# Weight sums of the retention's value and gate projections: by accumulating loads in place of vector additions, with the seven products reordered

## The chip, the cores and the metric

The kernel runs on one core of a Trainium2 chip. Its metric is the device time of one execution in microseconds. The engines named below are PE (the matrix engine), DVE (vector), ACT (activations), POOL and SP; SP issues the loads and stores of the kernel before.

## The reference

Two layers over 1024 tokens of width 1024, in float32. The first is a retention with four heads, each with 256 query and key columns and 512 value and gate columns; the second is a stick-breaking attention with eight heads. Cut to what the change touches, the first layer is:

```python
u = rms_norm(h, ret_norm_pre[i])
proj = u @ ret_w_in[i]
q, k, v, g = jnp.split(proj, [...], axis=-1)
q = rope(split_heads(q)); k = rope(split_heads(k)) * (RET_QK_DIM ** -0.5)
o = retention_chunkwise(q, k, v)
o = (o - mu) * lax.rsqrt(var + EPS)
o = merge_heads(o) * jax.nn.silu(g)
y = o @ ret_w_out[i]
h = h + rms_norm(y, ret_norm_post[i])
```

The change is in how `v` and `g` are computed from `u` and their weights.

## The kernel before, in words

The tokens are taken in two halves of 512. The retention is done for each half in turn (phases A, t = 0 and 1), then the attention for each half (phases C). Every float32 operand of a matmul is kept as two tiles of reduced precision, a high and a low part; `split` (L574) makes them with one ACT copy (L577) and one DVE subtraction (L578), and `mm3` (L412) issues three matmuls (L415, L416, L417) for a product. A load of weights brings 128 partitions of 512 floats, 256 KB, into a raw tile (`raw_w`, L342, a ring of six `wraw` buffers in phases A); two such raw tiles are split into one block of weights in a `whl` tile, of which there are three.

In a phase A each head u runs three main pieces of work: `qk`, the projection to queries and keys; the output projection of the head before (`outproj`); and `vg` (L770), the projection to values and gates. `vg` runs for seven of the eight heads (the first head of the first half uses plain projections). `vg` splits the tokens of the half (256 and 256), the 1024 input columns (512 and 512) and the output columns (values and gates) each in two, and computes the 2 by 2 block product with seven block products instead of eight. The products are numbered 1 to 7. Each has two weight blocks, i = 0 and 1, and each block serves two K tiles of 128 and two token blocks: 12 matmuls a block, 24 a product. Some products take a loaded block of weights as it is (1, 2, 4), others sums of blocks, made by DVE before the split: for product 5 the sum of two gate blocks (L797), for 6 that sum less a value block (L800), for 3 a value block less the last sum (L803), for 7 a gate block less that sum (L806). The running sum lies in the two `S` tiles (L781). The tokens' sums are made once per half by `sums` (L630).

The products share PSUM banks. Products 1, 6 and 7 accumulate in one pair of banks, 5 and 3 in a second pair, 2 in a third and 4 in a fourth; after a product whose bank goes on accumulating, ACT copies the bank out (`copy`, L821), and `plus` (L825) adds such a copy to another bank's content, which gives the values (`vput`) and gates (`gput`). The order of the products is written out at L828 as 1, 2, 5, 6, 3, 7, 4.

Beside a main piece run side pieces: `scores` (query times key, masked by POOL at L892), `mix` (scores times values, with a normalisation whose small steps run on POOL at L938, L939 and L940) and `gate` (product with the gates, transposed by PE at L983). The order of every engine's queue is not the program's: `arrange` (L101) simulates all engines with a cost per instruction (`_time`, L68), tries five rounds of priorities (`latest`, `justify`, `place`), and fixes the best order found on all five queues. Each queue then runs in order, each instruction waiting for what it needs.

Of the kernel before, what the change touches and what calls it, by code (L numbers as in the profile page):

```python
# [37 lines left out]
BACKLOG = 3000.0  # L38
HAND = {"PE": 100.0, "DVE": 60.0, "Activation": 60.0, "Pool": 100.0, "SP": 50.0}
# [28 lines left out]
def _time(s, chip):  # L68

    n = _size(s.outs[0])  # L70
    if s.eng == "PE":
        full = str(s.ins[0].dtype) == "dt.float32" and not s.turns
        t = max(216.0, n * 5 / 3 + 26.0) if full else max(110.0, n / 2.4 + 13.5)
        return t, t + 165.0
    bank = any(b.tensor.name in chip.banks for b in s.ins)
    if s.eng == "DVE":
        two = sum(_size(b) == n for b in s.ins) > 1
        if s.op == "InstTensorTensor":
            t = (n + 143) / 0.96
# [18 lines left out]
    return n * 512 / 330.0, 4000.0  # L98


def arrange(nc, tc, tag_of, bufs, banks, turns):  # L101
# [4 lines left out]
    for ins in nc.cur_bb.bb.instructions:  # L106
# [8 lines left out]
        s.turns = bool(getattr(ins, "is_transpose", False))  # L115
        s.before, s.after, s.behind, s.next = set(), set(), set(), set()
# [21 lines left out]
        s.shares = s.eng == "Pool" or s.eng == "DVE" and sum(b.tensor.name not in banks for b in s.ins) > 1  # L138
# [45 lines left out]
def justify(steps, order, follow):  # L184
# [8 lines left out]
    for s in sorted(steps, key=lambda s: (-s.end, -s.k)):  # L193
# [9 lines left out]
        busy = max(s.busy, 400.0) if s.eng == "SP" else s.busy  # L203
# [11 lines left out]
def place(steps, users, tags, tag_of, bufs, rank):  # L215
# [41 lines left out]
    for _ in range(n):  # L257
# [51 lines left out]
def trunk(ctx, tc, xT, wts, gains, trig, ident_in, cols, out):  # L309
# [52 lines left out]
    keep = tc.keep_in_program_order  # L362
# [121 lines left out]
    def outproj(base, oT, y_d, first, acc=None, tags=None):  # L484
# [11 lines left out]
        def chunk(j):  # L496
# [110 lines left out]
    def a_prep(t):  # L607
# [22 lines left out]
        def sums(i):  # L630
# [95 lines left out]
    class AHead:  # L726
# [19 lines left out]
        def gput(self, tb, src):  # L746
            g = self.sg[tb] = S("sg", [512])
            A_.activation(g[:], src, AF.Sigmoid)
            V.tensor_tensor(g[:], src, g[:], ALU.mult)
# [12 lines left out]
        def first_g(self):  # L762
            self.sg = [None] * 4

# [5 lines left out]
        def vg(self):  # L770
# [3 lines left out]
            self.v, self.sg = [None] * 4, [None] * 4  # L774
            box = {"S": [None, None]}

            def left(n, i):
# [4 lines left out]
                for c in range(2):  # L782
                    cl = slice(512 * c, 512 * c + 512)

                    def load(which, kk):
                        raw = raw_w()
                        dma(raw, wts[base + 4 + 4 * which + kk, :, cl])
                        return raw

                    s = box["S"][i][:, cl] if box["S"][i] else None  # L790
                    if n == 1:
                        src = load(0, i)
                    elif n == 2:
                        src = load(0, 2 + i)
                    elif n == 5:
                        a, b, src = load(1, i), load(1, 2 + i), s
                        V.tensor_tensor(src, a, b, ALU.add)  # L797
                    elif n == 6:
                        a, src = load(0, i), s
                        V.tensor_tensor(src, src, a, ALU.subtract)  # L800
                    elif n == 3:
                        src = load(0, 2 + i)
                        V.tensor_tensor(src, src, s, ALU.subtract)  # L803
                    elif n == 7:
                        a, src = load(1, 2 + i), s
                        V.tensor_tensor(src, a, src, ALU.subtract)  # L806
                    else:
                        src = load(1, 2 + i)
# [19 lines left out]
            order = [(n, i) for n in (1, 2, 5, 6, 3, 7, 4) for i in range(2)]  # L828
            get = ahead(14, lambda at: left(*order[at]))

            def chunk(n, i, kk):
                if kk == 0:
# [4 lines left out]
                    if i == 0:  # L837
                        first = {1: "ma", 2: "o", 5: "mb", 4: "mb"}.get(n)
# [11 lines left out]
                for tb, p in enumerate(banks):  # L850
# [8 lines left out]
                    elif n == 7:  # L859
                        self.gput(tb, plus(box[5, tb], p))  # L860
                    else:
                        self.gput(2 + tb, plus(box[7, tb], p))
# [3 lines left out]
        def out(self, y_d, acc=None, tags=None):  # L866
            return outproj(self.base + 12, lambda: self.oT, y_d, self.h == 0, acc, tags)
# [625 lines left out]
    def run():  # L1493
# [12 lines left out]
        for ip, (kind, t) in enumerate(phases):  # L1506
# [5 lines left out]
            for u in range(4):  # L1512
                ring[:] = rings(kind, t, u)
                if kind == "A":
# [20 lines left out]
                    else:  # L1535
# [9 lines left out]
                       [([], 0, 0) if 0 < u < 3 else (H.scores(), 3, 15), (H.begin(), 20, 0), (more, 4, 8)])  # L1545
# [112 lines left out]
```

## Time and profile before

| what | value |
|---|---|
| median of 3 runs | 1716.36 us (lowest 1715.91) |
| the profiled execution's own time | 1716.91 us |
| its span, first to last instruction | 1714.8 us |
| PE busy | 1700.1 us, 8057 matmuls |
| DVE busy | 1308.4 us |
| ACT busy | 880.9 us |
| POOL busy | 142.8 us |
| moved by DMA | 348.78 MB, all of the program's own on SP's queue |

The busy times are the unions of an engine's instructions, so that overlapping matmuls are counted once. A row of the timeline gives the start of an instruction in microseconds from the span's start, its length, the engine, the line, what it writes and reads, and in brackets the idle time of the engine just before it with what ended it. A row of a group gives the busy time of all its instructions and the mean nanoseconds of one.

### The profile page before, as it was taken

How to read it: one execution, taken by the hardware profiler on the slowest of the kernel's cores; microseconds unless marked ns; L12 is line 12 of the kernel's file. 1: busy time of each engine (PE TensorE's matmuls, PEld its weight loads, DVE VectorE, ACT ScalarE, POOL GpSimd, SP SyncE). 2: the span in 40 equal slices, each digit the busy share in tenths (PEclk: the TensorE clock that was granted, in tenths of full speed). 3: DMA queues.
4: the chain of work that ended last, by engine and by line, in shares of the span. 5: the costliest groups of instructions: out<-in, count | busy, mean ns of one | idle time of the engine just before them, and what ended most of it. 6: DMA issues, size and time to landing. Idle time of an engine off the chain costs nothing.

```text
span 1714.8 us, 23975 instructions
## 1 busy us (share of the span) xinstructions
PE 1700.1 (99%) x8057; PEld 1419.0 (83%) x8057; DVE 1308.4 (76%) x2213; ACT 880.9 (51%) x1646; POOL 142.8 (8%) x275
## 2 busy tenths in 40 slices
PE   9999999999999999999999999999999999999997
PEld 7888888888888888878888888888888888888887
DVE  8856868889867978688888778667887756656865
ACT  6435536555545535355655544544674445445643
POOL 0000101010010000101010100000001001001001
PEclk9999999999999999999999999999999999999999
DMA  5236475668545676376896999667883763463523
GB/s 187 98 105 203 148 236 185 203 193 271 187 146 176 225 240 209 98 256 209 291 320 198 332 314 308 209 209 257 280 292 111 252 225 101 160 219 99 162 95 125
DMA packets 182250, 348.78 MB, mean 203 GB/s; under 512 B 20208, under 2 KB 24432, under 8 KB 182128
## 3 DMA queue, kind: packets, MB, share of 16 engines
q1 hardware_dynamic: 182128, 347.26, 61.0%
q8 instruction: 63, 1.03, 0.2%
q14 instruction: 59, 0.48, 0.1%
HBM read 273.78 MB, written 73.40 MB: 202 GB/s over the span
## 4 chain that ended last, share of the span: by engine, by line
PE 99%; DMA 0%; DVE 0%; ACT 0%; issue 0%; SPq 0%; POOL 0%; DVEq 0%
PE pmb L415 13%; PE pmb L417 13%; PE pmb L416 13%; PE pma L415 12%; PE pma L417 12%; PE pma L416 12%; PE po L417 5%; PE po L416 5%; PE po L415 5%; PE pz L1355 2%; PE pz L417 2%; PE pz L416 2%; PE pz L415 2%; PE pz L983 1%; PE pz L551 0%; DMA S<-in_xT_dram 0%
## 5 line engine op out<-in xcount | busy, mean ns | idle before, releaser
L577 ACT ACTIVATE whl<-wraw 128x512 fp32r<-128x512 f32 x323 | 190.8, 625 | 203.4 <-PE pmb L417 80.4
L578 DVE TENSOR_TENSOR whl<-wraw,whl 128x512 fp32r<-128x512 f32 x323 | 214.3, 686 | 64.3 <-ACT whl L577 63.1
L415 PE MATMUL pma<-xh,whl 128*128 128x512 f32 x384 | 153.1, 399 | 0.0
L415 PE MATMUL pmb<-xh,whl 128*128 128x512 f32 x384 | 152.4, 397 | 0.0
L417 PE MATMUL pma<-xh,whl 128*128 128x512 f32 x384 | 150.1, 391 | 0.0
L417 PE MATMUL pmb<-xh,whl 128*128 128x512 f32 x384 | 150.0, 391 | 0.0
L416 PE MATMUL pma<-xh,whl 128*128 128x512 f32 x384 | 149.9, 390 | 0.0
L416 PE MATMUL pmb<-xh,whl 128*128 128x512 f32 x384 | 149.6, 390 | 0.0
L1325 DVE TENSOR_TENSOR_SCAN sgn<-sgn 128x384 f32<-128x384 f32 (+4 forms) x64 | 86.5, 1354 | 27.7 <-POOL sgn L1323 27.7
L580 ACT ACTIVATE whl<-wraw,gn 128x256 fp32r<-128x256 f32 (+1 forms) x144 | 80.4, 600 | 50.0 <-PE pmb L417 32.4
L577 ACT ACTIVATE AT<-pz 128x512 fp32r<-128x512 f32 (+1 forms) x96 | 46.3, 487 | 108.0 <-PE pz L1355 105.9
L1322 POOL TENSOR_SCALAR_AFFINE_SELECT A<-A 128x128 f32<-128x128 f32 x64 | 33.1, 516 | 775.1 <-ACT A L1317 775.1
L578 DVE TENSOR_TENSOR AT<-pz,AT 128x512 fp32r<-128x512 f32 (+1 forms) x96 | 52.9, 555 | 57.6 <-ACT AT L577 57.1
L581 DVE SCALAR_TENSOR_TENSOR whl<-wraw,gn,whl 128x256 fp32r<-128x256 f32 (+1 forms) x144 | 82.0, 601 | 17.1 <-ACT whl L580 16.5
L415 PE MATMUL pmb<-oT,whl 128*128 128x512 f32 x240 | 94.9, 396 | 0.0
L417 PE MATMUL pmb<-oT,whl 128*128 128x512 f32 x240 | 93.8, 391 | 0.0
L416 PE MATMUL pmb<-oT,whl 128*128 128x512 f32 x240 | 93.7, 391 | 0.0
L577 ACT ACTIVATE whl<-S 128x512 fp32r<-128x512 f32 x104 | 63.0, 628 | 48.1 <-PE pmb L417 12.5
L417 PEld LDWEIGHTS pmb<-xh,whl 128*128 128x128 f32 x384 | 72.1, 188 | 15.8
L417 PEld LDWEIGHTS pma<-xh,whl 128*128 128x128 f32 x384 | 72.1, 188 | 15.6
L416 PEld LDWEIGHTS pmb<-xh,whl 128*128 128x128 f32 x384 | 72.2, 188 | 13.5
L415 PEld LDWEIGHTS pmb<-xh,whl 128*128 128x128 f32 x384 | 72.2, 188 | 13.4
(389 smaller groups left out, 4614.0 us busy)
## 6 DMA issues: line engine op xcount, KB each, us to landing
wraw<-in_wts_dram SPq DMA_DIRECT2D x522, 256.0 KB, 3.6
y<-f SPq DMA_DIRECT2D x120, 256.0 KB, 3.2
f<-y SPq DMA_DIRECT2D x88, 256.0 KB, 4.1
S<-in_wts_dram SPq DMA_DIRECT2D x44, 256.0 KB, 4.1
vo<-in_wts_dram SPq DMA_DIRECT2D x42, 256.0 KB, 4.3
ko<-in_wts_dram SPq DMA_DIRECT2D x40, 256.0 KB, 4.4
T<-AT SPq DMA_DIRECT2D x32, 256.0 KB, 4.7
sc<-T SPq DMA_DIRECT2D x16, 512.0 KB, 5.1
```

The source lines that it names most:

```text
L415: MM(p, lh, rh, start=start, stop=False, **kw)
L416: MM(p, lh, rl, start=False, stop=False, **kw)
L417: MM(p, ll, rh, start=False, stop=stop, **kw)
L577: A_.activation(dst[0], src, AF.Copy)
L578: V.tensor_tensor(dst[1], src, f32(dst[0]), ALU.subtract)
L580: A_.activation(dst[0], src, AF.Copy, scale=scale)
L581: V.scalar_tensor_tensor(dst[1], src, scale, f32(dst[0]), ALU.mult, ALU.subtract)
L983: nc.tensor.transpose(pt[:, 128 * e:128 * e + 128], on[:, 128 * e:128 * e + 128], ident[:])
L1322: first = G.affine_select(a[:, dg], a[:, dg], [[-1, 128]], ALU.is_gt, 0.0, base=0, channel_multiplier=1)
L1325: V.tensor_tensor_scan(n[:, :W][:, ::-1], n[:, :W][:, ::-1], n[:, :W][:, ::-1], 1.0, ALU.mult, ALU.bypass)
L1355: nc.tensor.transpose(p[:, 128 * tb:128 * tb + 128], self.A[hh][tb][:, c0:c0 + 128], ident[:])
```

## The change

The additions of weight blocks leave DVE. A raw block is loaded into the sum's tile by SP, and a further block is added to it by a load that POOL issues and that accumulates into its destination (`plus_dma`). So that sums suffice, the signs of two of the four token sums are turned (`sums`). For product 5 the sum is gate block 1 plus gate block 2; for 6 value block 1 is added to it, for 3 value block 2 is added to that; for 7 a value block is loaded into a `wraw` tile and a gate block accumulated on it. The gates then come out with the opposite sign: `gput` applies the sigmoid with a factor of -1, and the output projection of such a head subtracts its result instead of adding it. The order of the products becomes 5, 1, 2, 6, 7, 3, 4; the banks of 5 and 3 change places with those of 1, 6 and 7. The first steps of `mix` are placed in the last four of the 28 chunks of `vg` instead of the last eight. The planner gets costs for loads issued by POOL, and takes into account that a bank read by two engines is read by one after the other.

```diff
+HOLD = {"SP": 400.0, "Pool": 1100.0}
...
+    if s.moves:
+        return n * 512 / 330.0, 4000.0 if s.eng == "SP" else 6000.0
...
-            s.before |= {o.k for o, n, w in last[name] if w and n & m}
+            s.before |= {o.k for o, n, w in last[name] if n & m and (w or name in banks and o.eng != s.eng)}
...
-        if e == "SP":
-            ring_free = max(t + 1000.0, ring_free) + busy * 1.05
-            end, busy = ring_free + 1550.0, 400.0
+        if s.moves:
+            ring_free = max(t + 600.0 + HOLD[e], ring_free) + busy * 1.05
+            end, busy = ring_free + (3100.0 if e == "Pool" else 1550.0), HOLD[e]
...
+    def plus_dma(dst, src):
+        nc.gpsimd.dma_start(dst, src, accum_op=ALU.add)
...
             if first:
-                A_.activation(y[:], p[:], AF.Copy)
+                A_.activation(y[:], p[:], AF.Copy, scale=-1.0 if turned() else 1.0)
+            elif turned():
+                V.tensor_tensor(y[:], y[:], p[:], ALU.subtract)
...
-            V.tensor_tensor(a[:, 0], q[0], q[1], ALU.subtract)
-            V.tensor_tensor(a[:, 1], q[2], a[:, 0], ALU.subtract)
+            V.tensor_tensor(a[:, 0], q[1], q[0], ALU.subtract)
+            V.scalar_tensor_tensor(a[:, 1], a[:, 0], -1.0, q[2], ALU.mult, ALU.subtract)
             V.tensor_tensor(b[:, 0], q[2], q[0], ALU.subtract)
-            V.tensor_tensor(b[:, 1], q[3], a[:, 1], ALU.subtract)
+            V.scalar_tensor_tensor(b[:, 1], a[:, 1], -1.0, q[3], ALU.mult, ALU.subtract)
...
-                    s = box["S"][i][:, cl] if box["S"][i] else None
+                    src = box["S"][i][:, cl] if n in (5, 6, 3) else raw_w()
                     if n == 1:
-                        src = load(0, i)
+                        dma(src, at(0, i))
                     elif n == 2:
-                        src = load(0, 2 + i)
+                        dma(src, at(0, 2 + i))
                     elif n == 5:
-                        a, b, src = load(1, i), load(1, 2 + i), s
-                        V.tensor_tensor(src, a, b, ALU.add)
+                        dma(src, at(1, i))
+                        plus_dma(src, at(1, 2 + i))
                     elif n == 6:
-                        a, src = load(0, i), s
-                        V.tensor_tensor(src, src, a, ALU.subtract)
+                        plus_dma(src, at(0, i))
                     elif n == 3:
-                        src = load(0, 2 + i)
-                        V.tensor_tensor(src, src, s, ALU.subtract)
+                        plus_dma(src, at(0, 2 + i))
                     elif n == 7:
-                        a, src = load(1, 2 + i), s
-                        V.tensor_tensor(src, a, src, ALU.subtract)
+                        dma(src, at(0, i))
+                        plus_dma(src, at(1, i))
                     else:
-                        src = load(1, 2 + i)
+                        dma(src, at(1, 2 + i))
...
-            order = [(n, i) for n in (1, 2, 5, 6, 3, 7, 4) for i in range(2)]
+            order = [(n, i) for n in (5, 1, 2, 6, 7, 3, 4) for i in range(2)]
...
-                        first = {1: "ma", 2: "o", 5: "mb", 4: "mb"}.get(n)
+                        first = {5: "ma", 1: "mb", 2: "o", 4: "mb"}.get(n)
...
-                        self.gput(tb, plus(box[5, tb], p))
+                        self.gput(tb, plus(box[5, tb], p), -1.0)
...
-                       [([], 0, 0) if 0 < u < 3 else (H.scores(), 3, 15), (H.begin(), 20, 0), (more, 4, 8)])
+                       [([], 0, 0) if 0 < u < 3 else (H.scores(), 3, 15), (H.begin(), 24, 0), (more, 4, 8)])
```

More of the change, by code (lines that the diff above doesn't have):

```diff
@@ L97, in _time @@
         return t, t
-    return n * 512 / 330.0, 4000.0
 def arrange(nc, tc, tag_of, bufs, banks, turns):
@@ L115, in arrange @@
         s.turns = bool(getattr(ins, "is_transpose", False))
+        s.moves = s.eng == "SP" or "DMA" in s.op
         s.before, s.after, s.behind, s.next = set(), set(), set(), set()
@@ L137, in arrange @@
         s.busy, s.whole = _time(s, chip)
-        s.shares = s.eng == "Pool" or s.eng == "DVE" and sum(b.tensor.name not in banks for b in s.ins) > 1
+        s.shares = s.eng == "Pool" and not s.moves or s.eng == "DVE" and sum(b.tensor.name not in banks for b in s.ins) > 1
         steps.append(s)
@@ L202, in justify @@
         line = taken[s.eng]
-        busy = max(s.busy, 400.0) if s.eng == "SP" else s.busy
+        busy = HOLD[s.eng] if s.moves else s.busy
         i = bisect.bisect(line, (t, t))
@@ L482, in proj, with outproj @@
         return Chunks([lambda j=j: chunk(j) for j in range(16)], lambda: get(0))
-    def outproj(base, oT, y_d, first, acc=None, tags=None):
+    def outproj(base, oT, y_d, first, acc=None, tags=None, turned=lambda: False):
         box = {}
@@ L744, in vput, with gput @@
             split((x[:, 0, :], x[:, 1, :]), src, c)
-        def gput(self, tb, src):
+        def gput(self, tb, src, sign=1.0):
             g = self.sg[tb] = S("sg", [512])
-            A_.activation(g[:], src, AF.Sigmoid)
+            A_.activation(g[:], src, AF.Sigmoid, scale=sign)
             V.tensor_tensor(g[:], src, g[:], ALU.mult)
@@ L763, in first_g @@
             self.sg = [None] * 4
+            self.turned = False
             def evac(n, bg):
@@ L774, in vg @@
             self.v, self.sg = [None] * 4, [None] * 4
+            self.turned = True
             box = {"S": [None, None]}
```

11 lines of the change are left out of this document (4 added, 7 removed).

## The prediction

> **What bounds the kernel now.** I read the page's busy times, slices and chain first, then who PE waited for, then the windows around each wait.
>
> ```profile
> span 1714.8 us, 23975 instructions
> ...
> PE 1700.1 (99%) x8057; PEld 1419.0 (83%) x8057; DVE 1308.4 (76%) x2213; ACT 880.9 (51%) x1646; POOL 142.8 (8%) x275
> ...
> PE   9999999999999999999999999999999999999997
> ...
> PE 99%; DMA 0%; DVE 0%; ACT 0%; issue 0%; SPq 0%; POOL 0%; DVEq 0%
> ```
>
> ```profile
> PE pz L415 <- ACT qk L577: 1.8, 1, 1.8
> ```
>
> ```profile
> core 0: us, PE busy (x) PEld busy (x) DVE busy (x) ACT busy (x) POOL busy (x), PEclk, DMA share, GB/s
> 0.00:9.50 9.50, 6.49 (x16) 4.24 (x16) 2.89 (x8) 4.61 (x8) 0.20 (x4) 1.00 0.68 200
> 720.00:740.00 20.00, 18.18 (x78) 14.64 (x77) 17.21 (x32) 7.23 (x13) 0.41 (x1) 0.91 0.48 157
> 740.00:900.00 160.00, 160.00 (x737) 133.17 (x736) 137.16 (x242) 92.45 (x169) 15.81 (x24) 1.00 0.81 272
> 1690.00:1714.80 24.80, 15.02 (x124) 14.52 (x122) 13.85 (x29) 8.76 (x19) 8.27 (x7) 0.84 0.24 85
> ```
>
> The chain is PE from end to end. Of the 14.7 us in which PE idles, 3.0 lie in the first 9.5 us, 9.8 in the last 24.8 and 1.8 in one wait in the middle; 160 us stretches like the fourth row have none. A busy PE could still be a slow one, so I look at the pitch inside one `vg` (first half, second head): the start of its first product, of its second, of product 6 and of the one after it.
>
> ```profile
> 143.60 0.39 PE L415 MATMUL pma<-whl,xh 128*128 128x512 f32 x1
> 149.04 0.39 PE L415 MATMUL po<-whl,xh 128*128 128x512 f32 x1
> 159.92 0.39 PE L415 MATMUL pma<-whl,A 128*128 128x512 f32 x1
> 165.36 0.39 PE L415 MATMUL pmb<-whl,xh 128*128 128x512 f32 x1
> ```
>
> A product's 24 matmuls take 5.44 us, 227 ns each, and the spacing never slips. The change neither adds nor removes a matmul (seven products of 24 before and after, the output projection only changes sign). So nothing of DVE's or ACT's load is on the path; what can be won is the one wait in the middle, and what can be lost is any new wait of PE.
>
> **What is removed.** DVE loses the four groups of sums:
>
> ```profile
> L797 DVE TENSOR_TENSOR S<-wraw,wraw 128x512 f32<-128x512 f32 x28 | 19.1, 686 | 11.7 <-DMA wraw<-in_wts_dram 11.6
> L800 DVE TENSOR_TENSOR S<-S,wraw 128x512 f32<-128x512 f32 x28 | 18.9, 691 | 0.0
> L806 DVE TENSOR_TENSOR S<-wraw,S 128x512 f32<-128x512 f32 x28 | 18.8, 682 | 0.3 <-DMA wraw<-in_wts_dram 0.3
> L803 DVE TENSOR_TENSOR wraw<-wraw,S 128x512 f32<-128x512 f32 x28 | 18.6, 682 | 0.0
> L581 DVE SCALAR_TENSOR_TENSOR whl<-wraw,gn,whl 128x512 fp32r<-128x512 f32 x66 | 47.9, 746 | 12.7 <-ACT whl L580 12.1
> ```
>
> That is 112 instructions, 19.1 + 18.9 + 18.8 + 18.6 = 75.4 us, so DVE falls to about 1233. All of it lies beside PE: gain on the path 0. The sixteen token sums that become scalar_tensor_tensor cost at most 746 - 686 = 60 ns more each, 1 us on DVE, on the path 0 (DVE has some 24% of its time free to hide it; were it not hidden it would be that 1 us). The turned signs of gate and output projection replace operations one for one: 0. SP loses 12 of 32 issues in a `vg` and its loads become shorter in number: 0, since PE waits for no load now.
>
> **What is added: loads that accumulate.** Sixteen per `vg` (four each for 5, 6, 3, 7), 112 in all, issued by POOL; with the 20 left on SP there are 36 loads in place of 32, 28 x 256 KB or 7.3 MB more in all. DMA engines have room (0.81 busy in the fullest stretch above). Their cost on the path is 0 if they land before the split needs them, so I work out the room from the rows of product 6's first block before, which PE needs at 159.92:
>
> ```profile
> 154.73 1.32 ACT L577 ACTIVATE whl<-S 128x512 fp32r<-128x512 f32 x2 [1.09 <-PE po L417]
> ```
>
> ```profile
> 155.39 0.69 DVE L578 TENSOR_TENSOR whl<-S,whl 128x512 fp32r<-128x512 f32 x1
> 156.60 0.69 DVE L578 TENSOR_TENSOR whl<-S,whl 128x512 fp32r<-128x512 f32 x1
> ```
>
> The split starts 5.2 us before its matmuls (the third `whl` buffer came free then) and ends 2.6 us before them. A sum may be added to once its old value is split, and must be there when the next split starts. For links d products apart the room is thus 5.44 d - 5.2 + 2.6, and PE waits only after 2.6 us more. From 5 to 6 (d = 3): 13.7 and 16.3. From 6 to 3 (d = 2): 8.3 and 10.9. Product 7 goes through `wraw`: by the ring of six, its first block gets the buffers of product 1's second block, free at about product 1's start + 0.1; its split starts 3 x 5.44 - 5.2 = 11.1 after that start, so load and accumulation together have 11.0 us, or 13.6 before PE waits. Product 5 is made while the previous output projection runs, with no old value to wait for.
>
> No accumulating load is in the trace, nor any load issued by POOL. The nearest rows:
>
> ```profile
> wraw<-in_wts_dram SPq DMA_DIRECT2D x522, 256.0 KB, 3.6
> ...
> v<-v SPq DMA_DIRECT2D x16, 512.0 KB, 6.3
> ```
>
> ```profile
> 134.76 0.41 POOL L892 TENSOR_SCALAR_AFFINE_SELECT sc<-sc 128x256 fp32r<-128x256 f32 x1 [1.36 <-DVE sc L578]
> 179.99 0.54 POOL L938 TENSOR_TENSOR small<-small,cc 128x1 f32<-128x1 f32 x1 [44.83 <-DVE small L934]
> ...
> 289.14 2.14 POOL L939 TENSOR_TENSOR small<-small,mhalf 128x1 f32<-128x1 f32 x1
> ```
>
> From below it is the plain load, 3.6 us (nothing makes it faster than that, it moves the same bytes and reads its destination besides); from above the slowest 512 KB transfer plus the slowest small step of POOL, 6.3 + 2.1 = 8.4. I take 6.3, the 512 KB row, since it touches twice the bytes. Then the sum for 3 has 8.3 - 6.3 = 2.0 us to spare without delaying anything, and 7 has 11.0 - 3.6 - 6.3 = 1.1; even 8.4 stays inside 13.6 - 3.6 = 10.0. Cost 0; with the cover gone it is what the next part but one prices.
>
> What is queued behind a waiting accumulation on POOL: in this `vg` POOL has nothing to do for 44.8 us before 179.99, so only the loads themselves. Outside it, the masks (L892) stand before the next `vg`'s sums, and the normalisation (L938 to L940) after product 3's, which are due before product 4 starts. PE waits for neither soon. SP's queue gets shorter and is passed by nothing.
>
> **What is moved: the order of products.** Two effects. First, 7 now follows 6 at once in the same banks, so PE may not write a bank until ACT has copied product 6 out. In the trace 6 ended when 3 began (165.36), and its copies ran:
>
> ```profile
> 164.88 0.60 ACT L821 ACTIVATE f<-pma 128x512 f32<-128x512 f32 x1 [0.84 <-PE pma L417]
> ...
> 166.67 0.58 ACT L821 ACTIVATE f<-pma 128x512 f32<-128x512 f32 x1
> ```
>
> The first copy ends at 165.48, 0.12 after PE wants that bank; the second bank is wanted 3 x 0.227 later, at about 166.2, and was copied by 167.25 because a split stood in between on ACT. So the price is between 0 (other matmuls in between, or all of one bank first) and 1.2 us per `vg`. I take 0.17, the first copy's 0.12 with a small handoff: nobody waited for the second copy in the trace, now PE does, and the planner's priorities go by what waits. 7 x 0.17 = 1.2 us. Second, product 3, which completes the first values, moves one place back, and mixing can start up to 5.4 us later. Its end has cover:
>
> ```profile
> 200.62 0.76 ACT L952 ACTIVATE sgn<-po,small,small 128x512 f32<-128x512 f32 x1
> ...
> 203.44 0.60 PE L983 MATMUL pz<-ident,sgn 128*128 128x128 f32 x4
> 212.12 0.39 PE L415 MATMUL pma<-oT,whl 128*128 128x512 f32 x1
> ```
>
> From the last normalised block (201.4) to the first matmul that reads the gated result are 10.7 us, in which a DVE product (0.69, like the rows of that size above), four transposes (0.60) and a split (0.60 and 0.69) must be done, 2.6 us, or 4 with handoffs; 6.7 us are to spare, more than 5.4. Cost 0; without that cover up to 5.4 per head.
>
> **The sum.** The profiled execution took 1716.91 us, 2.1 of it outside its span. 1716.91 + 0 + 1.2 = 1718.1. The median of the runs is 0.55 lower than this execution, so I expect a median of **1717.6 us**.
>
> **The rivals.**
> *The middle wait goes.* PE waited 1.82 us at 732.33:
>
> ```profile
> 731.08 0.68 DVE L722 TENSOR_TENSOR f<-f,f 128x512 f32<-128x512 f32 x1
> 731.66 1.14 ACT L577 ACTIVATE qk<-f 128x512 fp32r<-128x512 f32 x2
> 732.33 0.50 PE L415 MATMUL pz<-qk 128*128 128x512 f32 x1 [1.82 <-ACT qk L577]
> ```
>
> The clock granted in that window was 0.91, which lost another 0.09 x 20 = 1.8 us. All queues are ordered anew, so it may vanish: 1717.6 - 1.2 - 3.6 = 1712.8. Against it: none of the removed sums stands in its chain (the rotary steps and ACT's splits), the first of them comes ten microseconds later. Chance 0.12.
>
> *Banks collide.* The change's two products between links hold for 5 and 6 and not for 6 and 7, so it would not do what it says: at 1.2 us for each of seven calls 8.4 in place of 1.2, 1724.8. For it speaks that the ACT queue did put a split between the two copies; against it, that nothing was in a hurry then. Chance 0.12.
>
> *The accumulations land late (slower than before).* Place: product 7 of each `vg`. From a landing time x of 10.0 us PE waits x - 10 in each of seven calls, and each idle microsecond costs about another by the clock (1.8 lost beside 1.82 above): 14 (x - 10). At 11 us 14 more, 1732; the 2% bound, 34 us, is reached at x = 12.5; at 13 us 42, 1760. A wait at 7 also gives product 3 the same time, so it does not pay again. For it: the kind of load is unseen; against it: 10 us is 2.8 times the plain load and more than any row. Chance 0.10, half of it beyond 2%. The Trainium skill, in "TensorE: Matmul & The Clock Gate", Part 1, says that the clock falls only after an idle window of about 3.4 us; by it the price would be half, 7 (x - 10). Here 1.82 us of idleness went with a clock of 0.91, so the measurement decides.
>
> *DVE holds POOL off.* POOL's small step of 0.5 us once took 2.14 (the row at 289.14), beside a busy DVE. If POOL could issue only when DVE pauses, it would wait as long as DVE runs on, which in this `vg` was from the first of these rows to the idle time before the second:
>
> ```profile
> 152.28 0.69 DVE L797 TENSOR_TENSOR S<-wraw,wraw 128x512 f32<-128x512 f32 x1 [0.43 <-DMA wraw<-in_wts_dram]
> 161.84 0.69 DVE L578 TENSOR_TENSOR whl<-wraw,whl 128x512 fp32r<-128x512 f32 x1 [0.32 <-ACT whl L577]
> ```
>
> That is 9.2 us, x = 15.5, 14 x 5.5 = 77, 1795. Against it: the step lost 1.6 us, not nine, and the removed sums open gaps. Chance 0.04. The rule that speaks for it is the Trainium skill's "SBUF — State Buffer", section "SBUF: two separate sides", its warning that DVE blocks DMA: while DVE holds the shared port in a two-port mode, POOL cannot write the descriptors of its loads. No run here shows such a load yet.
>
> **How the numbers follow.** My forecast (1715 to 1721) has 0.62, the others 0.12, 0.12, 0.10 and 0.04. The range 1712 to 1735 leaves out the far half of the late loads and the held-off POOL (0.09) and some of the first rival's lower end (0.04). A change of this kernel under 2% (34 us) is what I count as none. Faster by that would need 34 us where PE idles 14.7: 0.01. Slower: 0.05 + 0.04 = 0.09. Within: 0.90.
>
> **What would show it.** PE should have 8057 matmuls and be busy about 1700 us; L797 to L806 without DVE work and DVE near 1233; a second DMA queue with 112 issues, landing in 4 to 8.4 us; PE waits for ACT's copies under 1.2 us each, and none for a split of a summed block. The forecast falls if PE waits for splits of S or `wraw` in `vg`, if the landing time is above 10 us, or if the granted clock dips in windows of `vg`.

## The result, and the profile after

The kernel with the change took 1733.07 us (median of four runs, 1732.51 to 1733.81), beside 1716.13 us for the kernel before on the same chip: a ratio of 1.0102, 95% interval 1.0082 to 1.0122. The 1716.13 is the median of four runs, one of which took 3299.96 us; that one is left out of the ratio. The change is 17 us slower, half of the 2% that was counted as a change. The forecast was 1717.6, in a main case of 1715 to 1721; the range reached to 1735.

The page of the changed kernel begins so (busy times, then the shares of the chain that ended last):

```profile
span 1732.1 us, 24080 instructions
...
PE 1706.7 (99%) x8057; PEld 1419.0 (82%) x8057; DVE 1246.0 (72%) x2101; ACT 879.0 (51%) x1646; POOL 234.4 (14%) x387
...
PE 92%; DMA 3%; DVE 2%; issue 1%; ACT 1%; SPq 0%; POOL 0%; DVEq 0%; ACTq 0%; POOLq 0%
```

PE does the same 8057 matmuls. It is idle for 1732.1 - 1706.7 = 25.4 us, against 14.7 before, and its busy time is 6.6 us longer: 10.7 + 6.6 = 17.3, the whole difference of the two spans. The chain, 99% PE before, now runs through DMA, DVE and ACT for some per cent.

Whom PE waited for (total us, times, longest us), the groups that are new or larger:

```profile
PE pmb L420 <- ACT f L826: 4.2, 2, 2.2
PE po L420 <- ACT v L587: 3.4, 2, 1.8
PE po L421 <- DVE v L588: 1.9, 3, 0.8
...
PE pz L420 <- ACT qk L584: 0.8, 1, 0.8
```

And where, from the timeline of PE (the bracket is the idle time before the instruction and what ended it):

```profile
180.91 0.47 PE L420 MATMUL po<-v,sc 128*128 128x512 f32 x1 [1.55 <-ACT v L587]
...
288.22 0.47 PE L420 MATMUL po<-v,sc 128*128 128x512 f32 x1 [1.82 <-ACT v L587]
...
583.86 0.50 PE L420 MATMUL pmb<-whl,A 128*128 128x512 f32 x1 [2.17 <-ACT f L826]
587.08 0.79 PE L420 MATMUL pmb<-whl,A 128*128 128x512 f32 x1 [2.03 <-ACT f L826]
```

So there are two main kinds of new wait, none longer than 2.2 us: `mix` waits for the values that product 3 completes (`v`), and product 7 waits for the copies of product 6 (`f`, L826), in a few of the seven `vg` calls and not in all. Five waits for splits (`whl`, L585) add 1.4 us, none above 0.4. The old wait in the middle shrank from 1.8 us to 0.8 and 0.3. The stretches just around three of these waits, in the view by windows:

```profile
core 0: us, PE busy (x) PEld busy (x) DVE busy (x) ACT busy (x) POOL busy (x), PEclk, DMA share, GB/s
180.00:185.00 5.00, 3.55 (x9) 2.67 (x10) 5.00 (x11) 3.00 (x5) 1.36 (x2) 0.72 1.09 291
288.00:294.00 6.00, 5.23 (x22) 4.12 (x23) 5.59 (x11) 3.55 (x8) 1.80 (x4) 1.00 1.10 289
584.00:590.00 6.00, 3.97 (x11) 2.88 (x12) 2.19 (x4) 2.26 (x4) 2.60 (x3) 0.59 0.99 239
```

The granted clock (the column after POOL) fell to 0.72 and 0.59 around the waits at 180 and at 584 to 587 us, and stayed at 1.00 around the one at 288. The two windows lost 0.28 x 5 + 0.41 x 6 = 3.9 us by that, and the windows just behind them (185 to 190 at 0.93, 590 to 596 at 0.85) another 1.3. The kernel before lost 1.8 us in the middle. So at most about 3.4 of the 6.6 us of longer busy time are the clock's; what made the rest is not shown.

The new loads themselves do what was expected of them (median us from issue to landing, from the page):

```profile
S<-in_wts_dram POOLq DMA_DIRECT2D x84, 256.0 KB, 6.5
...
wraw<-in_wts_dram POOLq DMA_DIRECT2D x28, 256.0 KB, 6.8
```

The 6.3 us of the forecast's working was nearly right. What was not foreseen is *when POOL sends them*. Its timeline in the first `vg` of the changed kernel, products 7 (`wraw`) and 3 (`S`):

```profile
151.47 1.76 POOL L366 DMA_DIRECT2D wraw<-in_wts_dram  x2 [10.06 <-DMA wraw<-in_wts_dram]
153.97 0.86 POOL L366 DMA_DIRECT2D wraw<-in_wts_dram  x1 [0.74 <-DVE whl L585]
156.63 0.88 POOL L366 DMA_DIRECT2D wraw<-in_wts_dram  x1 [1.79 <-DVE whl L585]
160.90 0.88 POOL L366 DMA_DIRECT2D S<-in_wts_dram  x1 [3.39 <-DVE f L830]
162.90 0.86 POOL L366 DMA_DIRECT2D S<-in_wts_dram  x1 [1.13 <-DVE v L588]
164.44 0.86 POOL L366 DMA_DIRECT2D S<-in_wts_dram  x1 [0.68 <-DVE whl L585]
167.42 0.87 POOL L366 DMA_DIRECT2D S<-in_wts_dram  x1 [2.11 <-issue]
```

Product 3's sums need only the splits of product 6, which DVE had finished by 159.3, and yet the four loads leave at 160.90, 162.90, 164.44 and 167.42. The trace also has each load's landing. The loads of 151.47, 152.15, 153.97, 156.63 and 160.90 landed at 156.32, 160.59, 162.60, 164.14 and 167.11: product 7's fourth load and all four of product 3's left 0.3 us after the load three places earlier had landed. In the whole trace no more than three accumulating loads are ever under way, and 34 of the 112 leave in this way, 0.31 us after a landing that left two under way. The names in the brackets are only the events nearest in time (a DVE instruction that POOL does not need); the last row says it openly with "issue". What that did to ACT, the timeline of ACT in the same place:

```profile
167.19 0.63 ACT L584 ACTIVATE whl<-S 128x512 fp32r<-128x512 f32 x1 [1.12 <-DMA S<-in_wts_dram]
169.86 0.63 ACT L584 ACTIVATE whl<-S 128x512 fp32r<-128x512 f32 x1 [2.04 <-DMA S<-in_wts_dram]
...
173.24 0.63 ACT L584 ACTIVATE whl<-S 128x512 fp32r<-128x512 f32 x1 [0.84 <-DMA S<-in_wts_dram]
...
180.04 1.34 ACT L587 ACTIVATE v<-f,cc 128x512 fp32r<-128x512 f32 x2 [1.41 <-DVE f L830]
```

Four splits of product 3 wait for their sums (the one not shown, at 171.76, for 0.78 us), everything behind them on ACT and DVE moves back, and `v` is made at 180.04, when PE already stands waiting for it.

### The profile page after: what moved, and what is told of

Its sections match the earlier page's. It is cut to its first block, busy times and chain, and to the rows that moved or that the text cites. A ratio compares the mean times of both kernels' runs of the same rounds, so it can differ in the third digit from the quotient of the medians.

```text
span 1732.1 us, 24080 instructions
## 1 busy us (share of the span) xinstructions
PE 1706.7 (99%) x8057; PEld 1419.0 (82%) x8057; DVE 1246.0 (72%) x2101; ACT 879.0 (51%) x1646; POOL 234.4 (14%) x387
## 4 chain that ended last, share of the span: by engine, by line
PE 92%; DMA 3%; DVE 2%; issue 1%; ACT 1%; SPq 0%; POOL 0%; DVEq 0%; ACTq 0%; POOLq 0%
PE pmb L420 12%; PE pmb L422 12%; PE pmb L421 12%; PE pma L420 11%; PE pma L421 11%; PE pma L422 11%; PE po L421 5%; PE po L422 5%; PE po L420 5%; PE pz L1360 2%; PE pz L422 2%; PE pz L421 2%; PE pz L420 1%; DMA S<-in_wts_dram 1%; DMA vo<-in_xT_dram 1%
## 5 line engine op out<-in xcount | busy, mean ns | idle before, releaser
L585 DVE TENSOR_TENSOR whl<-wraw,whl 128x512 fp32r<-128x512 f32 x322 | 214.1, 687 | 87.5 <-ACT whl L584 86.6
L585 DVE TENSOR_TENSOR whl<-S,whl 128x512 fp32r<-128x512 f32 x104 | 69.8, 690 | 68.6 <-ACT whl L584 68.4
L366 POOL DMA_DIRECT2D S<-in_wts_dram x84 | 75.1, 935 | 245.3 <-DVE whl L585 86.8
L585 DVE TENSOR_TENSOR AT<-pz,AT 128x512 fp32r<-128x512 f32 (+1 forms) x96 | 52.9, 555 | 61.5 <-ACT AT L584 60.6
L422 PEld LDWEIGHTS pmb<-xh,whl 128*128 128x128 f32 x384 | 72.1, 188 | 15.7
```

The costliest lines, as they stand in the source:

```text
L366: nc.gpsimd.dma_start(dst, src, accum_op=ALU.add)
L422: MM(p, ll, rh, start=False, stop=stop, **kw)
L585: V.tensor_tensor(dst[1], src, f32(dst[0]), ALU.subtract)
```

## The experiments

Ratios are against the kernel before, run on the same chip; its median was 1715.5 to 1715.8 us throughout. Theory A, formed from the timeline above, is that the room in which POOL's loads keep their descriptors (the kernel gives it 1024 bytes a partition, `dynamic_dma_scratch_size`) holds only some three accumulating loads, so that POOL, whose queue is in order, stands still until an earlier one has landed.

**The room doubled.** The change as it is, with

```diff
-dynamic_dma_scratch_size=1024
+dynamic_dma_scratch_size=2048
```

> The changed kernel with twice the bytes kept for the descriptors of loads that POOL issues (2048 a partition in place of 1024); every queue has the same instructions in the same order. Theory A (room for descriptors: in the first vg call the issues of the sums for product 3 start at 160.90, 162.90, 164.44 and 167.42 us although the splits and loads that they wait for were over by 159.3; each starts about when the load issued three before it lands, so only three accumulating loads fit): POOL's holds with no releaser go, the sums land 3 to 8 us earlier, PE's waits for v, for copies of product 6 and for splits mostly go, 1715 to 1722 us. Theory B (the accumulating loads are slow in themselves, or DVE holds POOL off): nothing changes, 1731 to 1735. Theory C (the loss is the new order of the products: the bank handed from 6 to 7, and the values being finished one product later): 1728 to 1735.

Measured: 1723.18 us, 1.0043 [1.0028, 1.0057], a microsecond above theory A's range; ten of the seventeen microseconds come back from a number that no instruction mentions. Up to seven accumulating loads are now under way, and none leaves 0.31 us after a landing. But the sums land only a little sooner. In the first `vg` product 3's four loads leave 4.9 to 8.0 us earlier than in the change and land 1.7 to 2.5 us earlier (165.4 to 171.4 in place of 167.1 to 173.2), not the 3 to 8 expected: with more of them under way each takes longer, 7.8 us in the median of the `S` loads where it was 6.5. The longest of the new waits that are left (timeline of PE, and of ACT just before; waits for `v` add 1.6 us):

```profile
575.19 0.50 PE L420 MATMUL pmb<-whl,A 128*128 128x512 f32 x1 [1.31 <-ACT f L826]
578.30 0.50 PE L420 MATMUL pmb<-whl,A 128*128 128x512 f32 x1 [1.92 <-ACT f L826]
```

```profile
577.14 0.63 ACT L584 ACTIVATE whl<-wraw 128x512 fp32r<-128x512 f32 x1 [2.00 <-DMA wraw<-in_wts_dram]
577.67 0.58 ACT L826 ACTIVATE f<-pmb 128x512 f32<-128x512 f32 x1
```

Here the copy of product 6 is late because a split stands ahead of it in ACT's queue, and that split waits for product 7's accumulation (`wraw`).

**The room cut to 768.**

```diff
-dynamic_dma_scratch_size=1024
+dynamic_dma_scratch_size=768
```

> The changed kernel with 768 bytes a partition for those descriptors in place of 1024, all else the same. Theory A: room for two accumulating loads, sixteen a vg call at two per 6.5 us are 52 us in a call of some 40, so PE waits some 10 us a call and more with the clock: over 1790 us. Theories B and C: 1731 to 1735, as without the edit.

Measured: 1754.96 us, 1.0223 [1.0205, 1.0241]. The direction is that of theory A, and theories B and C, which expected no change, fall; the size is less than A said. At most two loads are under way, and 56 of the 112 leave 0.31 us after a landing; but a load of `S` now lands in 5.6 us where A reckoned with 6.5. PE now also waits for splits (the first row), in seven places:

```profile
PE pma L420 <- ACT whl L584: 7.2, 7, 2.2
PE pmb L420 <- ACT f L826: 6.6, 4, 3.5
```

**The order alone.** Order, banks, signs and planner as in the change; each accumulating load replaced by a plain load and a vector addition:

```diff
     def plus_dma(dst, src):
-        nc.gpsimd.dma_start(dst, src, accum_op=ALU.add)
+        raw = raw_w()
+        dma(raw, src)
+        nc.vector.tensor_tensor(dst, dst, raw, ALU.add)
```

> The changed kernel with its new order of products, signs and planner, but every accumulating load replaced by a plain load and a DVE addition (112 additions, 77 us of DVE, as before the change). Theory C (order): 1728 to 1735, with PE waits for copies of product 6 and for v as in the changed kernel. Theories A and B (the loads of POOL): 1713 to 1720, PE waits as in the kernel before.

Measured: 1718.41 us, 1.0018 [1.0008, 1.0027]. At most 5 us, at least 1, are due to everything else in the change; no wait of PE for copies of product 6 or for `v` above 0.3 us is left. The loss is in the accumulating loads.

**The loads by themselves.** A small kernel, whose output is a copy of its input: POOL issues twelve plain loads of 256 KB, then three times twelve accumulating ones, the first with DVE idle; the second was meant to run beside additions of DVE, the third beside its copies.

```python
for i in range(N):
    keep(G.dma_start(P[i][:], wts[i, :, 512:1024]))
...
for i in range(N):
    keep(G.dma_start(A[0][i][:], wts[i, :, 512:1024], accum_op=ALU.add))
```

> None of the model is computed; the output is a copy of the input. Four groups of twelve 256 KB loads issued by POOL back to back, with 1024 bytes of descriptors: plain loads, accumulating loads, accumulating loads beside a stream of DVE additions with two operands in SBUF, and accumulating loads beside a stream of DVE copies. Theory A: plain loads go out seven or more before the first hold, accumulating ones three, and after that one for each that lands, a spacing of about 2.2 us. Theory B (slow loads): accumulating loads go out about 0.9 us apart without holds, and land over 6 us later. DVE holding POOL off: the third or fourth group has issues of well over 0.9 us, or holds that the second has not.

The timeline of POOL, start of the plain loads, then of the first accumulating ones:

```profile
57.30 4.48 POOL L44 DMA_DIRECT2D plain<-in_wts_dram  x8 [0.53 <-issue]
...
70.96 2.73 POOL L47 DMA_DIRECT2D sum<-in_wts_dram  x3 [0.39 <-issue]
75.14 0.85 POOL L47 DMA_DIRECT2D sum<-in_wts_dram  x1 [1.46 <-issue]
77.14 0.87 POOL L47 DMA_DIRECT2D sum<-in_wts_dram  x1 [1.15 <-issue]
...
89.28 0.86 POOL L47 DMA_DIRECT2D sum<-in_wts_dram  x1 [1.23 <-issue]
```

Eight plain loads go out back to back, but only three accumulating ones; the fourth to twelfth follow every (89.28 - 75.14) / 8 = 1.77 us. By the landings at most seven plain loads were under way (the first landed at 60.41, before the eighth left at 61.20) and at most three accumulating ones, and each that was held left 0.3 us after a landing. The groups of the three trials (busy us, mean ns | idle before), and the timeline of DVE:

```profile
L51 POOL DMA_DIRECT2D sum<-in_wts_dram x12 | 10.5, 958 | 8.8 <-issue 8.8
L57 POOL DMA_DIRECT2D sum<-in_wts_dram x12 | 10.5, 955 | 8.9 <-issue 8.9
L47 POOL DMA_DIRECT2D sum<-in_wts_dram x12 | 10.5, 960 | 9.1 <-issue 9.1
```

```profile
94.72 43.66 DVE L53 TENSOR_TENSOR z<-x,y 128x512 f32<-128x512 f32 x60
138.69 50.77 DVE L59 COPY z<-y 128x512 f32<-128x512 f32 x110
```

DVE's additions ran beside both L51 (issued from 94.84 to 113.8) and L57 (118.56 to 137.6), and they make no difference. The copies began when the last load had been issued, so no run here shows a load issued beside them. The rival that DVE holds POOL off falls for additions. In the changed kernel, too, an accumulating load's issue lasted 0.94 us in the mean, beside a DVE that was busy 72% of the time.

**The same with 2048 bytes**, to tell the room from a slow destination.

```diff
-SCRATCH = 1024
+SCRATCH = 2048
```

> The small kernel of loads alone again, with 2048 bytes a partition for the descriptors of POOL's loads in place of 1024; its output is a copy of the input, and nothing of the reference is computed. Theory A (the room for descriptors holds a certain number of accumulating loads): with 1024 bytes three of them went out back to back and then one every 1.75 us; with twice the room six or seven go out back to back at about 0.6 to 1 us each, and only the rest of the twelve are held. Theory B (the accumulation itself is slow at its destination, so that the spacing of 1.75 us is the transfer's own rate): again three back to back, then the same holds, 9 us of them in twelve.

```profile
68.63 8.95 POOL L47 DMA_DIRECT2D sum<-in_wts_dram  x10 [0.26 <-issue]
77.88 0.86 POOL L47 DMA_DIRECT2D sum<-in_wts_dram  x1 [0.31 <-issue]
```

Ten stand in one row of the timeline, so it is the room. At most seven were under way at once, as expected: the eighth, ninth and tenth left at 72.60, 74.52 and 75.96, each just after one of the first three had landed (72.35, 74.27, 75.56). The landings that follow come every 1.3 us (77.62 to 88.18, eight steps), where one load left every 1.77 us with the small room. "DMA: Bandwidth & Descriptors" of the Trainium skill, sections "Terms" and "The descriptor swizzle", has 16 bytes a descriptor and 9 + 9 descriptors per engine for one transfer of 1 MiB to 128 partitions. An estimate from that page, 288 bytes a load if one of 256 KB has as many, gives two loads in 768 bytes, three in 1024 and seven in 2048. The traces agree for accumulating loads. They do not for plain ones, of which seven were under way with 1024 bytes; if the room is what limits these too, a plain load takes less of it.

**Product 7's sum back on DVE, with the larger room.**

```diff
                         dma(src, at(0, i))
-                        plus_dma(src, at(1, i))
+                        raw = raw_w()
+                        dma(raw, at(1, i))
+                        V.tensor_tensor(src, src, raw, ALU.add)
```

> The changed kernel with 2048 bytes of descriptor room, and with product 7's sum made by a vector addition of two plain loads; only the chain of 5, 6 and 3 accumulates (84 loads on POOL in place of 112). Theory A1 (what the larger room left, 1723 against 1718 of the reordered kernel without accumulating loads, is product 7's load followed by its accumulation, two landings in a row): 1718 to 1720, and no wait of PE for copies of product 6 at about 575 and 578 us. Theory A2 (it is the chain's own accumulations, 3 above all): 1721 to 1724, with waits of PE for v in the windows of vg.

Measured: 1717.82 us, 1.0010 [1.0001, 1.0019]. A1 holds: the waits at 575 and 578 us are gone, and with them all but 2 us of the loss.

**The planner told of the holds**, 1024 bytes; and the same with 2048.

```diff
-HOLD = {"SP": 400.0, "Pool": 1100.0}
+HOLD = {"SP": 400.0, "Pool": 1800.0}
...
-            end, busy = ring_free + (3100.0 if e == "Pool" else 1550.0), HOLD[e]
+            end, busy = ring_free + (4500.0 if e == "Pool" else 1550.0), HOLD[e]
```

> The changed kernel with 1024 bytes of room as it is, but with the planner's costs of a load on POOL raised to what the small kernel showed: POOL held for 1.8 us by each (1.1 before), landing 4.5 us after its transfer (3.1 before). If the loss comes because the planner orders queues as if POOL could issue every 1.1 us, the waits of PE go for the most part: 1718 to 1725. If the room itself is the limit whatever the order (four sums need 7 us on POOL between the splits of 6 and those of 3): 1729 to 1736, as before.

> Both: 2048 bytes of room, and the planner's raised costs. If room and order are two separate causes: 1715 to 1719, at or a little above the kernel before (1716). If the order was of no account: 1723, as with the larger room alone. Below 1713 would need the one wait of PE in the middle of the kernel before to go as well.

Measured: 1725.97 us (1.0054 [1.0038, 1.0071]) and 1723.58 us (1.0042 [1.0027, 1.0057]). With the small room the costs are worth 7 us, and the time is 1 us above the span that was expected if the planner's costs were the cause: the waits for `v` sink from 5.3 us to 0.8. But POOL sends product 3's sums at 160.90, 162.98, 164.19 and 166.56, nearly as before: the order bends around the holds and does not remove them. With the large room the costs are worth nothing, so the two causes do not add, and that expectation failed: the new plan has another wait, 2.2 us for DVE in the output projection, which the larger room alone does not show.

**Product 7's sum back on DVE, small room.** The edit of the run with `plus_dma` taken out of product 7, now with 1024 bytes.

> The changed kernel with 1024 bytes of descriptor room, product 7's sum by a vector addition of two plain loads; the chain of 5, 6 and 3 accumulates as in the change (84 loads on POOL). Theory A (product 7's four accumulations fill the room just before product 3's, and POOL's queue is in order): with them gone at most four go out at a time, only the fourth of each group is held, and the time is 1717 to 1723 although the room is still 1024. Rival (the small room is the loss whoever uses it, four loads a group are one too many already): 1728 to 1734, with holds of POOL ahead of product 3's sums as before.

Measured: 1716.70 us, 1.0004 [0.9995, 1.0014]: the loss is gone without a byte more room. The issues of product 3's sums in the first `vg` (timeline of POOL) answer those of the changed kernel:

```profile
155.33 1.87 POOL L366 DMA_DIRECT2D S<-in_wts_dram  x2 [14.94 <-DVE whl L585]
158.05 0.86 POOL L366 DMA_DIRECT2D S<-in_wts_dram  x1 [0.85 <-DVE whl L585]
160.94 0.88 POOL L366 DMA_DIRECT2D S<-in_wts_dram  x1 [2.03 <-DVE whl L585]
```

The first three leave when the splits of product 6 free their tiles, 155.33 to 158.05, instead of 160.90 to 164.44, and the four land 5.5 to 6.9 us earlier than in the change. The fourth is held (160.94 is 0.31 us after the first one's landing), and 13 loads of this trace leave so, without a loss: a hold costs nothing where PE does not come to wait for it. The chain of 5, 6 and 3 by accumulating loads therefore costs nothing here, and it is product 7's four accumulations, just ahead of product 3's in POOL's queue, that cost the time.

**The accumulating loads in the old order.**

```diff
-            order = [(n, i) for n in (5, 1, 2, 6, 7, 3, 4) for i in range(2)]
+            order = [(n, i) for n in (1, 2, 5, 6, 3, 7, 4) for i in range(2)]
...
-                        first = {5: "ma", 1: "mb", 2: "o", 4: "mb"}.get(n)
+                        first = {1: "ma", 2: "o", 5: "mb", 4: "mb"}.get(n)
```

> The accumulating loads of the change alone: the products and their banks in the order of before (1, 2, 5, 6, 3, 7, 4), 1024 bytes of room. By the prediction's formula for the room of a link, adjacent products (5 to 6, 6 to 3) have 5.44 us before PE waits, and a landing takes 6.5: at least 1.1 us for each of 14 links, up to 3 for the second block whose loads go out later, about doubled by the clock: 1745 to 1800. Rival (the order is of no account, the room for descriptors alone sets the loss): 1728 to 1738, as with the new order.

Measured: 1736.30 us, 1.0116 [1.0101, 1.0131]: no more than the change itself (the intervals overlap), so the rival's number came out and the formula's did not. But the waits are of the kind that the formula meant, for splits and not for copies:

```profile
PE pma L420 <- ACT whl L584: 3.7, 3, 1.9
PE pmb L420 <- ACT whl L584: 3.0, 3, 1.8
```

In this order a sum must land within one product, and PE waits for splits in six places, up to 1.9 us each; in the new order it waits for them 0.4 us at most. Whether these waits come from the order alone is not shown: 48 loads of this trace leave 0.31 us after a landing, held like those of the change, and the old order was not run with product 7's sum on DVE.

**Only product 7 accumulates**, the chain by vector additions, with 1024 and with 2048 bytes. `plus_dve` is the load and addition of the order-only kernel; the three calls for products 5, 6 and 3 use it.

```diff
-                        plus_dma(src, at(1, 2 + i))
+                        plus_dve(src, at(1, 2 + i))
...
-                        plus_dma(src, at(0, i))
+                        plus_dve(src, at(0, i))
...
-                        plus_dma(src, at(0, 2 + i))
+                        plus_dve(src, at(0, 2 + i))
```

> The complement of the run with product 7's sum by DVE: only product 7 accumulates by POOL's loads (28), the chain of 5, 6 and 3 is made by vector additions of plain loads; 1024 bytes of room. Theory A (both together fill the room; each alone has space): 1717 to 1722. Rival (product 7's load followed by its accumulation is late by itself, through SP's queue where the loads of the block after it are mixed in): 1722 to 1730, with PE waits for copies of product 6 at about 575 to 585 us.

> The kernel in which only product 7 accumulates by POOL's loads (28 of them, the chain of 5, 6 and 3 by vector additions; 1733 with 1024 bytes of descriptor room), now with 2048 bytes. Theory C (product 7 is late because a load and an accumulation stand one behind the other in the ring of six raw tiles, whatever the room; the room only delays the fourth of each group): 1726 to 1733, with splits on ACT still waiting for product 7's raw tiles ahead of the copies of product 6. Theory A (the fourth accumulation, held until the first has landed, is the whole delay): 1716 to 1721, and the four go out back to back with no such wait behind them.

Measured: 1733.26 us (1.0091 [1.0074, 1.0108]) and 1732.81 us (1.0104 [1.0087, 1.0121]). Theory A said 1717 to 1722 and 1716 to 1721, and falls as the whole story; the first rival's range, to 1730, was too low, and theory C's, 1726 to 1733, held: with only 28 accumulating loads, and with room for all four of a group, product 7 alone loses the same 17 us. With 2048 bytes the four go out nearly together, and ACT still waits for them (timelines of POOL, ACT and PE, second `vg`; the line numbers are five higher in this kernel):

```profile
262.50 1.92 POOL L366 DMA_DIRECT2D wraw<-in_wts_dram  x2 [17.44 <-DMA wraw<-in_wts_dram]
264.69 1.77 POOL L366 DMA_DIRECT2D wraw<-in_wts_dram  x2 [0.27 <-issue]
...
273.86 0.63 ACT L589 ACTIVATE whl<-wraw 128x512 fp32r<-128x512 f32 x1 [1.52 <-DMA wraw<-in_wts_dram]
274.39 1.07 ACT L831 ACTIVATE f<-pmb 128x512 f32<-128x512 f32 x2
275.03 0.50 PE L425 MATMUL pmb<-whl,A 128*128 128x512 f32 x1 [2.88 <-ACT f L831]
```

POOL had waited 17.4 us for the plain load on which the accumulation is put. The order-only kernel (1718.41) differs from the first of the pair in product 7's sum alone, so there these 28 loads cost 15 us. This pair of kernels is harder on product 7 than the change is: the chain's blocks also go through the ring of six raw tiles, and the first accumulation of this `vg` leaves at 262.50 in place of 259.01. They show the mechanism (a load and an accumulation one behind the other in the ring), not its price in the change; that price is the 5 us between the change with 2048 bytes (1723.2) and the same with product 7 on DVE (1717.8).

## Why the prediction was right and wrong

That the time lies in the range is luck. The main case, 1715 to 1721, failed by 12 us; the range reached to 1735 only for the sake of the rival of late loads, whose mechanism is not the one that the traces show.

Shown by the runs, in sum: of the 17 us, about 10 go when the room is doubled and POOL is no longer held (1733 to 1723), 5 more when product 7's sum goes back to DVE, and 2 are the rest of the change (1717.8 then, 1715.8 before). All but that rest hangs on 28 of the 112 accumulating loads: without them the small room does no harm (1716.7).

- **PE bounds the kernel, nothing to gain.** Right: no variant was faster than the kernel before, and the 62 us taken off DVE bought nothing. Of all versions run, the one with product 7 on DVE is closest, and it is equal to the kernel before, not better.
- **DVE falls by 75.4 us.** Too much: 1308.4 - 1246.0 = 62.4, or 0.56 us for each of the 112 instructions. Their count was right (2213 to 2101). A group's busy time counts 0.67 us for each of them, but consecutive instructions of DVE start 0.60 us apart and overlap, mostly with those of other groups, and the page's busy time counts the overlap once.
- **Landing between 3.6 and 8.4 us, taken at 6.3.** Right: 6.5 and 6.8.
- **"POOL has nothing to do for 44.8 us ... so only the loads themselves."** This is the step that failed. The loads were given a landing time each and no limit on how many are under way. The step found only the loads themselves behind a waiting accumulation and put no price on that: product 3's four sums stand behind product 7's four. What the runs showed in its place is a limit of three under way, with 34 loads held until an earlier one had landed. The 2.0 us that the sum for 3 had to spare held for a load that leaves at once; in the first `vg` they left 5.6 to 6.6 us later than in the kernel with product 7 on DVE.
- **Product 7 has 1.1 us to spare** (11.0 - 3.6 - 6.3). Too optimistic in the same way. In the first `vg` of the second half, the timeline of POOL in the changed kernel shows two accumulations out, one of the chain, and then a hold:

```profile
572.86 1.78 POOL L366 DMA_DIRECT2D wraw<-in_wts_dram  x2 [11.55 <-DMA vo<-in_xT_dram]
575.79 0.86 POOL L366 DMA_DIRECT2D S<-in_wts_dram  x1 [1.15 <-DMA h<-vo]
580.49 0.88 POOL L366 DMA_DIRECT2D wraw<-in_wts_dram  x1 [3.83 <-issue]
```

  The third of product 7's loads left 7.6 us after the first, its split on ACT waited 2.10 us for it until 585.91, the copy of product 6 followed at 586.45, and PE's wait at 587.08 is the 2.03 us shown above.
- **7 after 6 in the same banks: 0.17 us per call.** Right where the loads do not interfere: without accumulating loads no wait for a copy is left, and with product 7 on DVE one of 0.8 us. The rival *banks collide* has its wait in the trace (4.2 us, `pmb` for `f`), but for another reason than the one given: not a split that happens to stand between two copies, but a split that waits for its data.
- **Mixing has 6.7 us of cover.** It has, at the end that was looked at, the gated result. The cover does not help at the other end: the first steps of `mix` stand in the last four chunks of `vg`, and PE stops there as soon as `v` is late, 3.4 + 1.9 = 5.3 us in all.
- **The rival of late loads** gave 1732 us, and its number came out; its mechanism did not. Its formula, 14 (x - 10), is zero for a landing of 6.8 us. What should have stood for x is the time from when a sum may be added to until it lands, of which the landing is only one part and the wait to be issued the other.
- **The middle wait goes.** It shrank from 1.8 to 0.8 + 0.3 us with the new order of the queues; no median shows a gain.
- **A lost microsecond costs another by the clock.** PE's busy time rose by 6.6 us for 10.7 of idleness, 0.6 each, and at most about half of that is traced to the clock; the forecast had 1. "TensorE: Matmul & The Clock Gate" of the Trainium skill, Part 1, has the clock fall after an idle window of about 3.4 us. This trace does not agree: the clock fell to 0.72 around waits of 1.55 and 0.54 us and to 0.59 around two of 2.17 and 2.03, and the measurement decides.
- **What would show it.** The listed signs were the right ones: the forecast was to fall if PE waits for splits of S or `wraw` or the clock dips in windows of `vg`. The second came true, and the first came true one step removed: ACT waits for the sums, and PE for what stands behind on ACT.

What stays open: why seven plain loads may be under way where three accumulating ones may; whether copies of DVE would hold POOL off; and how much of the smaller differences is the planner's, since every edit but that of the room orders all queues anew.

## What to carry to other kernels

Moving a sum from an engine into the load trades a duration for a queue: ask not only how long one such load takes to land but how many may be under way, how fast their landings follow one another, and what else stands behind the one that is held on the same in-order engine. An accumulation onto a tile that itself has to be loaded first puts two landings in a row into a prefetch that was deep enough for one; accumulating onto a running sum that is long there costs nothing here. And work taken off an engine that does not bound the kernel has no gain that could pay for such a risk.

## What the runs showed of the hardware

With 768, 1024 and 2048 bytes of room at most two, three and seven accumulating loads of 256 KB were under way, and a held one left 0.31 us after a landing in the kernels with 768 and 1024; of plain loads seven were under way with 1024. The issue of an accumulating load on POOL lasted 0.96 us in the mean, that of a plain one 0.57. With the small room a new accumulating load followed every 1.77 us, 262144 bytes / 1.77 us = 148 GB/s; with 2048 bytes they landed every 1.3 us, some 200 GB/s, while each took longer (8.9 us in the median, 5.0 with the small room). DVE's additions in float32 beside them changed neither the issue time nor the holds; its copies were not tried beside a load. And waits of about 2 us, well under a product's length of 5.4 us, went with a lower granted clock in two of three places and not in the third.
